# The high part of the mixers' weights: by a casting transfer on the gpsimd queue, or by a copy on the scalar or vector engine

## The chip, the cores and the metric

The kernel runs on one core of a Trainium2 chip. Its time is the device time of one execution in microseconds, from runs whose median is given. One execution was also taken by the hardware profiler; its page and trace are what this document reads. In the trace PE is TensorE's matmul, PEld its weight load, DVE is VectorE, ACT is ScalarE, POOL is GpSimd, SP is SyncE.

## What is computed

A two-layer network on 256 tokens of width 1024, in float32. Each layer is a half-weighted feed-forward block (SwiGLU, width 2816), a mixer, and another half-weighted feed-forward block, each followed by a residual sum with a factor and a layer normalisation:

```python
for layer in range(DEPTH):                      # DEPTH = 2, x: [1, 256, 1024]
    h = layer_norm(ALPHA * h + 0.5 * swiglu(h, ffn_w_in[layer, 0], ffn_w_out[layer, 0]), ...)
    if layer % 2 == 0:
        mix = hybrid_mixer(h, hyb_w_in, ..., hyb_w_out)      # [1024 x 5664] in, [2048 x 1024] out
    else:
        mix = nsa_mixer(h, positions, nsa_w_in, ..., nsa_w_out)  # [1024 x 1840] in, [1024 x 1024] out
    h = layer_norm(ALPHA * h + mix, ...)
    h = layer_norm(ALPHA * h + 0.5 * swiglu(h, ffn_w_in[layer, 1], ffn_w_out[layer, 1]), ...)
```

The hybrid mixer projects h, runs a causal convolution of length 4 over most of the columns, and then two branches beside each other: a gated delta rule (8 heads, solved in blocks) and a state-space scan (16 heads). Both are gated by a z projection and normalised, and go through one output projection. The NSA mixer is an attention of three branches (compressed blocks, selected blocks, window) with 16 query heads in 2 groups.

## The kernel before

**Three products for one.** TensorE runs the dense products in the type float32r, which keeps fewer bits than float32. To keep the accuracy, each dense weight tile is split in two: a high part `whi`, the weight rounded to float32r, and a low part `wlo`, the weight less its high part. The activations are split in the same way. A dense product is then three passes: high by high, high by low, low by high (`mm3`, lines 674 to 679).

**How a weight gets to TensorE.** `unit` (line 614) loads one weight unit of up to 128 x 2048 floats into a `raw` buffer by a transfer on SyncE's queue; there are 4 such buffers. It cuts the unit in parts of up to 128 x 1024 and for each part takes two buffers of the pool `m4`, `whi` and `wlo`, and calls `split` (line 608). `split` copies the part into `whi`, which rounds it. That copy is an operation with two possible engines: ScalarE's activation or VectorE's tensor_copy (`copy`, line 597). Then VectorE subtracts `whi` from the raw part into `wlo`. `unit_cols` (line 632) loads columns: each part is 128 columns for all 8 blocks of 128 rows, so in DRAM a partition's part lies in 8 runs of 512 bytes. `unit_rows` (line 638) loads rows of 512 or 1024 columns: a part is then 2 runs of 2 KB or 1 run of 4 KB for each partition. `tok_weights` (line 646) calls `unit_rows` for the z gates and the queries. The feed-forward blocks use `pair_weights` (line 654, with a split of its own) for their first tiles and `unit_cols` and `unit_rows` for the others. Two units of the mixers are loaded by direct calls of `unit`: the 32 small gate columns of the hybrid mixer (line 1068) and the key, value and gate columns of NSA (`chunk`, line 1578).

**Buffers.** `m4` has 36 buffers of 128 x 1024. Streams share it under quotas; the weight stream "W" may hold 12 while other streams have tiles pending that come before its own, and 24 otherwise. Within a stream, buffers are given in the order of first use in the program.

**What sets the order.** Nothing is issued directly. The program records operations in a `Plan`; `Plan.order` (line 315) then simulates a list schedule on five queues (tensor, vector, scalar, gpsimd, sync), with a price for each operation (`price`, line 239), latencies between engines, one shared DMA resource, buffers and PSUM banks. At each step it takes the operation that can start first, by program order where several can. An operation with two possible engines goes where it starts first. The result is one fixed order for each engine, which the hardware then follows with semaphores. So a change of a price or of an engine makes a new order for everything. Before, the price of every `dma_start` on its queue was 60 ns, and all were SyncE's.

**The mixers.** In the hybrid mixer the z gate of the delta branch (`z_gate`) and the key and query columns with their convolution (`gdn_conv`) come first; then five strands are woven by TensorE time (`weave`, line 729): the delta rule `delta`, the value columns and the state-space columns `space`, the second z gate `gate`, the scan `space2`, and the first half of the output projection `out_a`. The second half of it follows. GpSimd's part in it is small: triangular masks for the decays (`decays`, the tiles `bm`), inverse square roots by a power (`lnve` in the layer normalisation, `arena` elsewhere), and in NSA a few products (`tt`, which may also go to VectorE). No transfer is issued from GpSimd.

All operations are issued by one line (508), so the profile's lines are told apart by tile names, not by line numbers.

Of the kernel before, what the change touches and what calls it, by code (L numbers as in the profile page):

```python
# [9 lines left out]
F32 = mybir.dt.float32  # L10
# [3 lines left out]
OP = mybir.AluOpType  # L14
# [4 lines left out]
P = 128  # L19
# [142 lines left out]
class Plan:  # L162
# [76 lines left out]
    def price(self, op, eng, fn, args, kw):  # L239
        def n(a):  # L240
            return a.ids.size
        ps = lambda a: isinstance(a, V) and a.t.space == "PSUM"
        if eng == "tensor":
            out, l, r = args[:3]
            if fn == "transpose":
                return max(l.ids.size * 2, r.ids.size) / 2.4 + 2
            N, M = r.ids.size, l.ids.size
            if l.dtype == F32R:
                return N / 2.4 + (13.5 if M > 32 else 7)
            if M <= 32:  # L250
                return max(107.0, N * 0.42)
            if M <= 64:
                return 58.0 if N <= 64 else max(109.0, N * 0.84)
            return 4 * max(N, M) / 2.4 + 9
        if fn == "dma_start":
            return 60.0
        N = n(args[0]) if isinstance(args[0], V) else n(args[1])
        if isinstance(args[1] if len(args) > 1 else None, V):
            N = max(N, n(args[1]))
        ptr = sum(isinstance(kw.get(k), V) for k in ("scale", "bias"))  # L260
        if eng == "scalar":
            rows = args[0].p1 - args[0].p0

            more = (340 if rows <= 32 else 125 if rows <= 64 else 0) if fn == "activation" and N > 128 else 0
            return N / 1.2 + (51 if ps(args[1]) else 93) + 93 * ptr + (93 if "accum_out" in kw else 0) + more
        if eng == "vector":
            src = [a for a in args[1:] if isinstance(a, V)]
            if fn in ("tensor_copy", "tensor_scalar") and not any(ps(a) for a in src) and not ps(args[0]):
                c = N / (1.92 if N > 256 else 0.96) + 68
            elif fn == "reciprocal":  # L270
                c = N * 4 / 0.96 + 68
            elif fn == "memset":
                c = N / 0.96 + 20
            else:
                c = N / 0.96 + 67
            if fn == "scalar_tensor_tensor":
                c += 62 * isinstance(args[2], V)
            elif fn == "tensor_scalar":
                c += 62 * sum(isinstance(a, V) for a in args[2:4])
            return c  # L280
        if args[-1] is OP.pow:
            return 830.0 + 130.0 * N
        return max(250.0, {"tensor_tensor": N * 2.1 + 150, "memset": N * .83 + 36,
                           "affine_select": N * .9 + 180}.get(fn, N * 1.7 + 480))
# [247 lines left out]
class K:  # L532
# [78 lines left out]
        self.nc.vector.tensor_tensor(lo, src, hi.bitcast(F32), OP.subtract)  # L611


    def unit(self, srcs, parts):

        raw = self.plan.tile("raw", [P, 2048], F32, "raw", stream="W")
        for dst, src in srcs:
            self.nc.sync.dma_start(dst(raw), src)
        out = []
        for f in parts:  # L620
            v = f(raw)
            n = int(v.ids.size)
            shape = v.shape
            hi = self.m4(n, "whi", "W", F32R)
            lo = self.m4(n, "wlo", "W", F32R)
            if len(shape) == 3:
                hi, lo = (t.rearrange("p (a b) -> p a b", a=shape[1]) for t in (hi, lo))
            self.split(hi, lo, v)
            out.append((hi, lo))
        return out  # L630

    def unit_cols(self, w, c0, n):

        v3 = lambda r: r[:, :KD * n].rearrange("p (k n) -> p k n", k=KD)
        parts = [lambda r, e=e: v3(r)[:, :, e * P:(e + 1) * P] for e in range(n // P)]
        return self.unit([(v3, w[:, :, c0:c0 + n])], parts)

    def unit_rows(self, w, k0, nk, c0, n):

        v3 = lambda r: r[:, :nk * n].rearrange("p (k n) -> p k n", k=nk)  # L640
        g = min(nk, 1024 // n)
        out = self.unit([(v3, w[:, k0:k0 + nk, c0:c0 + n])],
                        [lambda r, e=e: v3(r)[:, e:e + g, :] for e in range(0, nk, g)])
        return [(hi[:, k, :], lo[:, k, :]) for hi, lo in out for k in range(g)]

    def tok_weights(self, w, c0, n):
# [187 lines left out]


    def ffn(self, l, j, x, then):
        nc = self.nc
        w_in = self.i['ffn_w_in'][l, j].rearrange("(k p) n -> p k n", p=P)
        w_out = self.i['ffn_w_out'][l, j].rearrange("(k p) n -> p k n", p=P)
# [7 lines left out]
        def gtiles(f):  # L847
            if f // 2 not in pairs:
                pairs[f // 2] = self.m4(1024, "g", "G", F32R).rearrange("p (a t) -> p a t", a=4)
            v = pairs[f // 2]  # L850
            return v[:, f % 2 * 2, :], v[:, f % 2 * 2 + 1, :]
# [55 lines left out]
        for s in range(NT, DFF // 256):  # L907
# [8 lines left out]
            for e in range(2):  # L916
                if e == 1:
                    wo = self.unit_rows(w_out, 2 * s, 2, 0, D)
                f = 2 * s + e
# [5 lines left out]
                g = gtiles(f)  # L925
# [105 lines left out]

    def hybrid(self, x, then):
        self.arena = None
        nc, i = self.nc, self.i
        V = nc.vector
        w_in = i['hyb_w_in'][0].rearrange("(k p) n -> p k n", p=P)
# [30 lines left out]
        v3 = lambda r: r[:, :256].rearrange("p (k n) -> p k n", k=KD)  # L1067
# [32 lines left out]
        g = self.sm([P, 2, 24], "g24")  # L1100
# [453 lines left out]

    def nsa(self, x, then):
        self.arena = None
        nc, i = self.nc, self.i
        V = nc.vector
        w_in = i['nsa_w_in'][0].rearrange("(k p) n -> p k n", p=P)
# [427 lines left out]
```

## Time and profile before

| | |
|---|---|
| Median of 3 runs | 1137.44 us (1136.66 to 1139.3) |
| Span of the profiled execution | 1135.9 us |
| Mean granted TensorE clock | 0.997 of full speed |
| Busy: PE / DVE / ACT / POOL | 1113.5 / 892.4 / 510.4 / 66.6 us |
| Bytes moved by DMA, mean rate | 198.37 MB, 175 GB/s |
| First feed-forward block | about 0 to 194 us |
| Hybrid mixer | about 194 to 446 us |
| Second and third feed-forward block | about 446 to 806 us |
| NSA mixer | about 806 to 945 us |
| Last feed-forward block | about 945 to 1136 us |

The profiled execution's own time is its span, from the first instruction to the last; it stands 1.5 us below the median of the runs, in which the launch and the end are counted too. A row of a group reads: line, engine, operation, output <- inputs by tile name, partitions x elements, xcount | busy time in us, mean ns of one | idle time of the engine just before them, and what ended it. A row of the chain reads: start in us, length in us, what. A row of the waits reads: who waited <- for whom: us in total, times, the longest. A row of the issues reads: destination <- source, queue, xcount, KB each, median us from issue to landing.

### The profile page before, as it was taken

How to read it: one execution, taken by the hardware profiler on the slowest of the kernel's cores; microseconds unless marked ns; L12 is line 12 of the kernel's file. 1: busy time of each engine (PE TensorE's matmuls, PEld its weight loads, DVE VectorE, ACT ScalarE, POOL GpSimd, SP SyncE). 2: the span in 40 equal slices, each digit the busy share in tenths (PEclk: the TensorE clock that was granted, in tenths of full speed). 3: DMA queues.
4: the chain of work that ended last, by engine and by line, in shares of the span. 5: the costliest groups of instructions: out<-in, count | busy, mean ns of one | idle time of the engine just before them, and what ended most of it. 6: DMA issues, size and time to landing. Idle time of an engine off the chain costs nothing.

```text
span 1135.9 us, 16503 instructions
## 1 busy us (share of the span) xinstructions
PE 1113.5 (98%) x6558; PEld 947.8 (83%) x6558; DVE 892.4 (79%) x1495; ACT 510.4 (45%) x909; POOL 66.6 (6%) x101
## 2 busy tenths in 40 slices
PE   9999999999999999999999999999999999999997
PEld 6888888898999778888888888888877668888886
DVE  7977778789979998777768967775869789777755
ACT  6644332378545655533333633342346556433320
POOL 1000000021011410000000000000101210000000
PEclk9999999999999999999999999999999999999999
DMA  9966552544632275755563765546336217655510
GB/s 331 337 209 207 188 198 84 177 131 128 220 123 75 78 268 175 257 198 180 185 215 112 270 211 188 188 153 190 111 105 229 75 40 270 238 194 185 185 38 37
DMA packets 150678, 198.37 MB, mean 175 GB/s; under 512 B 9389, under 2 KB 127562, under 8 KB 150602
## 3 DMA queue, kind: packets, MB, share of 16 engines
q1 hardware_dynamic: 150602, 197.33, 52.1%
q8 instruction: 51, 0.84, 0.3%
q14 instruction: 25, 0.20, 0.0%
HBM read 194.04 MB, written 1.05 MB: 172 GB/s over the span
## 4 chain that ended last, share of the span: by engine, by line
PE 88%; DVE 8%; ACT 2%; issue 1%; DMA 0%; POOL 0%; SPq 0%; DVEq 0%; ACTq 0%
PE ps L508 53%; PE acc L508 30%; PE mp L508 5%; DVE wlo L508 2%; DVE arena L508 1%; DVE cv L508 1%; DVE qs L508 1%; DVE P L508 1%; DMA raw<-in_ffn_w_in_dram 0%; ACT P L508 0%; DVE AT L508 0%; DVE h L508 0%; DVE x L508 0%; DVE whi L508 0%; DVE kd L508 0%
## 5 line engine op out<-in xcount | busy, mean ns | idle before, releaser
L508 DVE TENSOR_TENSOR wlo<-raw,whi 128x1024 fp32r<-128x1024 f32 (+1 forms) x349 | 416.7, 1214 | 8.6 <-ACT whi L508 5.7
L508 PE MATMUL ps<-x,whi 128*128 128x512 f32 (+1 forms) x1616 | 376.7, 363 | 0.7 <-ACT cv L508 0.5
L508 PEld LDWEIGHTS ps<-x,whi 128*128 128x128 f32 x1616 | 284.2, 188 | 45.8 <-ACT cv L508 1.8
L508 ACT ACTIVATE whi<-raw 128x1024 fp32r<-128x1024 f32 x255 | 256.9, 1049 | 15.8 <-DMA raw<-in_ffn_w_in_dram 10.5
L508 PE MATMUL acc<-whi,g 128*128 128x512 f32 x704 | 230.7, 391 | 0.0
L508 PE MATMUL ps<-x,wlo 128*128 128x256 f32 x1400 | 227.0, 283 | 1.5 <-DVE wlo L508 1.5
L508 ACT ACTIVATE sg<-ps 128x256 f32<-128x256 f32 x162 | 62.2, 384 | 352.3 <-PE ps L508 352.2
L508 PEld LDWEIGHTS ps<-x,wlo 128*128 128x128 f32 x1400 | 201.9, 190 | 14.0 <-DVE wlo L508 1.7
L508 DVE TENSOR_TENSOR sg<-ps,sg 128x256 f32<-128x256 f32 x162 | 68.7, 424 | 161.8 <-ACT sg L508 161.6
L508 PEld LDWEIGHTS acc<-whi,g 128*128 128x128 f32 x704 | 132.5, 188 | 25.9
L508 PE MATMUL acc<-wlo,g 128*128 128x512 f32 x352 | 138.1, 392 | 0.0
L508 PE MATMUL ps<-whi,x 128*128 128x512 f32 (+1 forms) x480 | 129.8, 386 | 1.2 <-DVE whi L508 1.2
L508 PEld LDWEIGHTS ps<-whi,x 128*128 128x128 f32 x480 | 86.1, 188 | 17.8 <-DVE whi L508 2.0
L508 PEld LDWEIGHTS acc<-wlo,g 128*128 128x128 f32 x352 | 66.4, 189 | 10.9
L508 PE MATMUL ps<-wlo,x 128*128 128x512 f32 (+1 forms) x240 | 68.0, 381 | 0.5 <-DVE wlo L508 0.5
L508 DVE CAST whi<-raw 128x1024 fp32r<-128x1024 f32 (+2 forms) x94 | 63.8, 681 | 5.0 <-DMA raw<-in_nsa_w_in_dram 3.9
L508 PE MATMUL acc<-whi,x 128*128 128x512 f32 x192 | 63.9, 403 | 0.1
L508 POOL TENSOR_TENSOR lnve<-lnve,mhalf 128x1 f32<-128x1 f32 x12 | 11.5, 957 | 706.4 <-DVE lnve L508 706.4
L508 PEld LDWEIGHTS ps<-wlo,x 128*128 128x128 f32 x240 | 43.2, 188 | 8.1 <-DVE wlo L508 1.2
L508 ACT ACTIVATE sg<-sg 128x256 f32<-128x256 f32 x74 | 30.9, 418 | 33.9 <-DVE sg L508 33.9
L508 DVE SCALAR_TENSOR_TENSOR cv<-cv,arena 128x255 f32<-128x255 f32 (+2 forms) x84 | 41.3, 494 | 1.3 <-ACT cv L508 0.6
L508 PEld LDWEIGHTS acc<-whi,x 128*128 128x128 f32 x192 | 35.5, 188 | 8.1 <-issue 1.1
(254 smaller groups left out, 1011.0 us busy)
## 6 DMA issues: line engine op xcount, KB each, us to landing
raw<-in_ffn_w_in_dram SPq DMA_DIRECT2D x74, 1024.0 KB, 5.1
raw<-in_ffn_w_out_dram SPq DMA_DIRECT2D x44, 1024.0 KB, 4.9
raw<-in_hyb_w_in_dram SPq DMA_DIRECT2D x20, 1024.0 KB, 5.1
raw<-in_ffn_w_in_dram SPq DMA_DIRECT2D x24, 512.0 KB, 4.3
raw<-in_hyb_w_out_dram SPq DMA_DIRECT2D x8, 1024.0 KB, 4.9
raw<-in_nsa_w_in_dram SPq DMA_DIRECT2D x5, 1024.0 KB, 5.0
raw<-in_nsa_cmp_w_dram SPq DMA_DIRECT2D x4, 1024.0 KB, 5.3
raw<-in_nsa_w_out_dram SPq DMA_DIRECT2D x4, 1024.0 KB, 7.6
```

The lines of the kernel that those rows point to most:

```text
L508: r = getattr(getattr(nc, eng), fn)(*[res(a) for a in args], **{k: res(a) for k, a in kw.items()})
```

## The change

In both mixers the high part of a dense weight no longer comes from the raw tile by a copy on ScalarE or VectorE. Instead, a transfer on GpSimd's queue reads the same weight from DRAM a second time and writes it into `whi`; as the destination is float32r and the source float32, the transfer converts. The low part is still VectorE's subtraction, now of the raw tile and the transferred high part. `unit_cols` and `unit_rows` pass the DRAM slices (`heads`). A flag `mixing` is set in the mixers and cleared in the feed-forward blocks, which keep the copy, as do the two direct calls of `unit`. The planner's price of a `dma_start` on GpSimd's queue is 1000 ns.

```diff
@@ Plan.price
         if fn == "dma_start":
-            return 60.0
+            return 1000.0 if eng == "gpsimd" else 60.0
@@ K
-    def unit(self, srcs, parts):
+    def unit(self, srcs, parts, heads=None):
 
         raw = self.plan.tile("raw", [P, 2048], F32, "raw", stream="W")
         for dst, src in srcs:
             self.nc.sync.dma_start(dst(raw), src)
         out = []
-        for f in parts:
+        for m, f in enumerate(parts):
             v = f(raw)
...
-            self.split(hi, lo, v)
+            if self.mixing and heads:
+                self.nc.gpsimd.dma_start(hi, heads[m])
+                self.nc.vector.tensor_tensor(lo, v, hi.bitcast(F32), OP.subtract)
+            else:
+                self.split(hi, lo, v)
             out.append((hi, lo))
         return out
@@ unit_cols
-        return self.unit([(v3, w[:, :, c0:c0 + n])], parts)
+        heads = [w[:, :, c0 + e * P:c0 + (e + 1) * P] for e in range(n // P)]
+        return self.unit([(v3, w[:, :, c0:c0 + n])], parts, heads)
@@ unit_rows
         out = self.unit([(v3, w[:, k0:k0 + nk, c0:c0 + n])],
-                        [lambda r, e=e: v3(r)[:, e:e + g, :] for e in range(0, nk, g)])
+                        [lambda r, e=e: v3(r)[:, e:e + g, :] for e in range(0, nk, g)],
+                        [w[:, k0 + e:k0 + e + g, c0:c0 + n] for e in range(0, nk, g)])
@@ ffn
+        self.mixing = False
@@ hybrid and nsa
+        self.mixing = True
```

More of the change, by code (lines that the diff above doesn't have):

```diff
@@ L1556, in nsa @@
         self.arena = None
+        self.mixing = True
         nc, i = self.nc, self.i
```

## The prediction

> **What bounds the kernel now.** I read the page's head first, then the stretches of time by stage, then the chain of waits in the two mixers, and last the groups, the waits and the issues.
>
> ```profile
> span 1135.9 us, 16503 instructions
> PE 1113.5 (98%) x6558; PEld 947.8 (83%) x6558; DVE 892.4 (79%) x1495; ACT 510.4 (45%) x909; POOL 66.6 (6%) x101
> q1 hardware_dynamic: 150602, 197.33, 52.1%
> ```
>
> TensorE is busy nearly all the time, so only time that TensorE loses can be won back. The span is 1135.9 us; the runs' median is 1137.44 us, 1.5 us more, and I carry these 1.5 us along. Next the stretches: the hybrid mixer runs from about 194 to 446 us, the NSA mixer from about 806 to 945 us.
>
> ```profile
> core 0: us, PE busy (x) PEld busy (x) DVE busy (x) ACT busy (x) POOL busy (x), PEclk, DMA share, GB/s
> 155.00:310.00 155.00, 153.57 (x1109) 137.76 (x1107) 133.98 (x283) 83.40 (x142) 13.07 (x12) 1.00 0.49 152
> 194.00:446.00 252.00, 249.62 (x1937) 219.84 (x1936) 228.95 (x437) 140.05 (x223) 39.29 (x51) 1.00 0.46 152
> 806.00:945.00 139.00, 129.39 (x816) 100.71 (x815) 113.19 (x211) 72.93 (x205) 16.70 (x21) 0.99 0.36 123
> ```
>
> TensorE stands visibly idle for 252 - 249.62 = 2.4 us in the hybrid mixer and 139 - 129.39 = 9.6 us in NSA: 12.0 us together. DVE is the second engine (229 of 252 us, 113 of 139 us), ACT has room, POOL is nearly free. The chain of waits in the same two stretches, hybrid first:
>
> ```profile
> by line: PE ps L508 38.7%; PE acc L508 27.6%; PE mp L508 8.7%; DVE wlo L508 6.0%; DVE cv L508 3.3%; issue 1.7%; DVE AT L508 1.7%; DVE arena L508 1.3%; DVE x L508 1.1%; DVE y L508 1.0%; DVE XT L508 0.9%; DVE kq L508 0.8%; ACT sw L508 0.8%; D
> by line: PE acc L508 23.7%; PE ps L508 23.2%; PE mp L508 17.2%; DVE qs L508 5.7%; DVE wlo L508 4.7%; DVE P L508 4.6%; DVE arena L508 4.3%; ACT P L508 3.3%; DVE kd L508 1.4%; DVE PT L508 1.4%; DVE whi L508 1.4%; issue 1.3%; DVE h L508 1.0%;
> ```
>
> The subtraction that makes the low part (wlo) is the largest piece that is not TensorE: 6.0% of 252 = 15.1 us and 4.7% of 139 = 6.5 us. The copy that makes the high part (whi) is hardly there.
>
> **The change, part by part.** How many copies go follows from the issues of the weights.
>
> ```profile
> raw<-in_hyb_w_in_dram SPq DMA_DIRECT2D x20, 1024.0 KB, 5.1
> raw<-in_hyb_w_out_dram SPq DMA_DIRECT2D x8, 1024.0 KB, 4.9
> raw<-in_nsa_w_in_dram SPq DMA_DIRECT2D x5, 1024.0 KB, 5.0
> raw<-in_nsa_w_out_dram SPq DMA_DIRECT2D x4, 1024.0 KB, 7.6
> raw<-in_hyb_w_in_dram SPq DMA_DIRECT2D x4, 512.0 KB, 3.6
> ```
>
> Each 1024 KB unit has two parts of 128x1024, each 512 KB unit one: 2 x 28 + 4 = 60 parts in the hybrid mixer and 2 x 9 = 18 in NSA, so 78 copies go and 78 transfers of 512 KB on POOL's queue come. The 32 gate columns and NSA's key and value chunks give no source for the high part and keep their copies. What the copies cost, hybrid first, then NSA (feed-forward weights prepared in these stretches are among them):
>
> ```profile
> L508 ACT ACTIVATE whi<-raw 128x1024 fp32r<-128x1024 f32 x49 | 50.1, 1050 | 5.6 <-DMA raw<-in_ffn_w_in_dram 4.1 <-PE ps L508 1.4
> L508 DVE CAST whi<-raw 128x1024 fp32r<-128x1024 f32 x15 | 10.7, 713 | 0.0
> L508 DVE TENSOR_TENSOR wlo<-raw,whi 128x1024 fp32r<-128x1024 f32 x64 | 77.9, 1227 | 0.9 <-ACT whi L508 0.5
> L508 ACT ACTIVATE whi<-raw 128x1024 fp32r<-128x1024 f32 x19 | 19.3, 1051 | 4.2 <-DMA raw<-in_nsa_w_in_dram 2.4 <-DMA raw<-in_nsa_w_out_dram 1.0 <-DMA raw<-in_ffn_w_in_dram 0.8
> L508 DVE CAST whi<-raw 128x1024 fp32r<-128x1024 f32 x7 | 4.8, 698 | 3.9 <-DMA raw<-in_nsa_w_in_dram 3.9
> ```
>
> ACT loses up to 50 + 19 us and DVE up to 10.7 + 4.8 us of work; the subtractions, 1.2 us each on the busier DVE, all stay. Most of what goes lies beside TensorE. What lies on the path: the copies in the chain, and TensorE's waits for ACT work that stands in the queue with such copies.
>
> ```profile
> 272.53 0.78 ACT whi L508
> 377.70 0.96 ACT whi L508
> 404.45 0.60 DVE whi L508
> 829.91 1.21 DVE whi L508 x2
> 862.03 0.69 DVE whi L508
> PE ps L508 <- ACT cv L508: 0.5, 1, 0.5
> PEld ps L508 <- ACT cv L508: 1.8, 5, 1.0
> PEld mp L508 <- ACT vT L508: 0.6, 1, 0.6
> PEld mp L508 <- ACT xT L508: 0.4, 1, 0.4
> ```
>
> **Gain.** The five pieces sum to 4.2 us; the waits to 3.3 us, of which I take half, since the convolution's own work ends them too. Together -6 us. The bounds are 0 and the 12.0 us that TensorE stands idle.
>
> **The later high part.** The copy yields the high part 1.05 us after its raw tile is there. A transfer can start when the slot is free, without the raw tile, but needs at least the 3.6 us of the 512 KB row: up to 3.6 - 1.05 = 2.55 us later wherever the slot came free only just in time. Who waits is wlo, and behind it in DVE's queue the convolution's sums, the delta rule and the normalisation. On the chain stand about 15.1 / 1.23 = 12 wlo in hybrid and 5 in NSA, 17 in all. The bounds are 0 (all fetched ahead) and 17 x 2.55 = 43 us.
>
> ```profile
> SPq L508 <- DVE wlo L508: 804.4, 149, 21.5
> 210.00:220.00 10.00, 10.00 (x60) 8.61 (x59) 5.41 (x7) 2.48 (x3) 0.00 (x0) 1.00 0.84 287
> 222.94 2.88 PE acc L508 x24
> L508 SPq DMA_DIRECT2D raw<-in_hyb_w_in_dram x18: 367/368/380, 196.7 to 306.8; - x18
> ```
>
> SyncE's queue waits 804 us in all for wlo to give back raw buffers, so fetching ahead is limited by buffers and not by transfers; yet the copies in hybrid waited for no raw tile of hybrid weights (their idle time names ffn_w_in alone). Nearer the low end, then: I let one in five of the 17 wait, about 3.5, and 3.5 x 2.55 = +9 us.
>
> **DMA share.** Queue q1 moves 197.33 MB in 52.1% of 1135.9 us: 333 GB/s at full share, so a part (128 x 1024 x 4 bytes = 0.524 MB) takes 1.57 us. Sixty take 94 us, and the hybrid share goes from 0.46 to 0.46 + 94 / 252 = 0.83. The 44 parts of the input projection (16 by rows for the two gates, 28 by columns), loaded between 155 and 310 us, take 69 us of 155: 0.49 + 0.45 = 0.94. That cover is nearly used up: raw tiles will land later than 5.1 us, and zero-fills and normalisation rows with them. At 0.84 (the stretch from 210 us) TensorE was still busy 10.00 of 10, so the price is small: I take +2 us, between 0 and the 10 us by which 0.94 of 155 us misses a full queue.
>
> **POOL's queue.**
>
> ```profile
> L508 POOL TENSOR_SCALAR_AFFINE_SELECT bm<-arena 128x512 fp32r<-128x512 f32 x24 | 22.3, 957 | 128.5 <-PE acc L508 67.4 <-DVE arena L508 39.0 <-PE ps L508 18.0
> L508 POOL TENSOR_TENSOR P<-P,arena 128x1024 f32<-128x1024 f32 x5 | 10.3, 2075 | 39.7 <-DVE arena L508 27.9 <-ACT PT L508 11.8
> L508 POOL TENSOR_TENSOR lnve<-lnve,mhalf 128x1 f32<-128x1 f32 x12 | 11.5, 957 | 706.4 <-DVE lnve L508 706.4
> ```
>
> No transfer is issued from POOL in this trace. The nearest rows bound an issue by SyncE's 0.37 us and by POOL's pass over 1024 columns, 2.08 us; I take 1 us, which is also what the planner is now told. 60 us fit beside 39.29 in 252. But POOL works in order: a transfer that waits for a slot holds up the decay masks (bm) and the powers (lnve, arena) behind it, and TensorE and DVE wait for those. One issue ahead of one power on the path: +1 us, between 0 and six powers at the borders of the mixers by 2.08 us, 12 us. SyncE's queue loses nothing and gets nothing.
>
> **The planner.** The new price of 1000 and the shorter ACT and DVE work give a new order on all engines. I set it at zero; by the idle of the mixers it can win no more than the 12.0 us.
>
> **Sum:** -6 + 9 + 2 + 1 = +6 us, and 1137.4 + 6 = 1143 us. Alone, this case reaches from 1140 to 1155.
>
> **A rule beside this.** The Trainium skill, "DMA: Bandwidth & Descriptors", section "Latency and other measured facts", puts the first byte of a transfer from SyncE or ACT at about 0.6 us and of one from GpSimd at about 1 us, since software writes its descriptors. By that estimate each of the 3.5 waits is 0.4 us longer and the sum is 1145 us; no trace here shows a GpSimd transfer yet.
>
> **Rivals.**
>
> **Faster, 1131 us.** The high parts are issued far enough ahead, since they need a slot but no raw tile, that no wlo on the chain waits. Only the gain stays, with the small terms hidden too: 1137.4 - 6. For it: POOL is free 84% of the hybrid stretch, and raw tiles of hybrid weights were never late. Against it: slots come free at TensorE's pace, and a high part now holds its slot some 2.5 us longer. It decides where fewer than 1.2 of the 17 wait (1.2 x 2.55 = 3 us, what the gain leaves after the two small terms).
>
> **POOL's issue becomes the bound, 1169 us.** A column part is 128 partitions by 8 rows: 1,024 runs of 512 bytes, where a row part has 128 or 256 runs. TensorE consumes a part in 2.88 us (24 products at 222.94). Were an issue of 1,024 runs longer than that, POOL would set the pace of the 28 column parts: at 4 us, 28 x 1.12 = 31 us. For it: the number of runs. Against it: the nearest rows end at 2.08 us. The Trainium skill, "SBUF — State Buffer", section "A bandwidth-pool intuition that's wrong (but worth ruling out)", adds that a DVE copy in its two-port mode keeps GpSimd from writing descriptors. One cast of 0.71 us per issue would lower the threshold to 2.17 us; but the 15 casts of the hybrid row mostly go with the change.
>
> **No change, 1137 us.** Waits and gain cancel, or the planner puts the freed time where TensorE has none to win. For it: TensorE busy 249.62 of 252.
>
> **How the numbers follow.** Forecast 0.36, POOL as the bound 0.16, faster 0.35, no change 0.13. A measurement here can tell about 0.2% (2.3 us) from nothing. Slower is the first two together, 0.52. The range goes down to 1128, the gain of 6 us and half of what it lacks to its bound, and up to 1170, the POOL case; outside I leave about 0.05 below and 0.10 above.
>
> **What would show it.** Right: about 78 transfers on a new queue of some 41 MB; ACT's whi groups in the two stretches down to the feed-forward and chunk weights; DMA share near 0.8 in hybrid; DVE idle ahead of wlo, released by the high part's transfer, some 10 us in sum; TensorE's hybrid stretch 4 to 8 us longer, NSA about even. Wrong toward faster: wlo waits for raw or for nothing. Wrong toward much slower: POOL busy over 2.9 us for a column transfer, or a high part that lands over 6 us after its issue even where the queue is quiet, which would mean that the casting itself is slow.

## The result, and the profile after

The changed kernel takes 1153.0 us (median of 4 runs, 1152.75 to 1153.83); before took 1137.8 us beside it (1136.66 to 1139.3). The ratio is 1.0137, with a 95% interval of 1.0125 to 1.0149: slower by 15 us. The profiled execution took 1153.1 us.

The head of the page of after:

```profile
span 1151.4 us, 16651 instructions
PE 1120.2 (97%) x6558; PEld 951.5 (83%) x6558; DVE 877.2 (76%) x1459; ACT 461.8 (40%) x863; POOL 119.3 (10%) x183
...
q1 hardware_dynamic: 150602, 197.33, 51.4%
q0 software_dynamic: 41184, 40.90, 16.7%
```

The change did what it says. ACT has 49 us less work and DVE 15 us less, and a new queue moves 40.90 MB (78 x 0.524). Yet TensorE, with the same 6558 products, is busy 6.7 us longer (1120.2 against 1113.5). Busy time of equal work grows only if single products get longer, so the clock has to be looked at.

Next the stretches of time, the two mixers from layer norm to layer norm, first before, then after (columns as in the prediction's rows):

```profile
197.70:441.60 243.90, 241.52 (x1897) 213.03 (x1897) 220.92 (x424) 137.08 (x217) 38.34 (x51) 1.00 0.46 150
812.10:949.90 137.80, 128.19 (x792) 98.71 (x791) 111.99 (x208) 71.75 (x200) 16.74 (x22) 0.99 0.38 131
```

```profile
198.10:461.90 263.80, 248.06 (x1897) 217.34 (x1896) 214.44 (x408) 103.32 (x182) 76.91 (x103) 0.97 0.99 242
832.40:963.50 131.10, 125.56 (x781) 95.74 (x780) 105.73 (x193) 65.95 (x197) 21.89 (x39) 1.00 0.61 197
```

The hybrid mixer lost 19.9 us (263.8 - 243.9), NSA won 6.7 us; part of that is a shifted border, since the stretch holds 781 products against 792. From NSA's first border to the end of the span, after is 4.8 us shorter (319.0 against 323.8). The four feed-forward blocks, from layer norm to layer norm, differ by 1.8 us together. Of the hybrid mixer's 19.9 us, 6.5 are TensorE's longer busy time (248.06 - 241.52, the same 1897 products), and 13.4 are idle time (15.7 against 2.4). The granted clock in the hybrid stage fell from 1.00 to 0.97. Where it fell, in stretches of 5 us of after:

```profile
305.00:310.00 5.00, 4.45 (x95) 3.83 (x95) 4.72 (x11) 1.68 (x5) 0.87 (x1) 1.00 1.31 322
310.00:315.00 5.00, 5.00 (x66) 4.94 (x63) 3.95 (x6) 0.00 (x0) 0.88 (x1) 0.53 1.92 315
315.00:320.00 5.00, 5.00 (x105) 4.52 (x105) 2.55 (x6) 0.98 (x2) 0.87 (x1) 0.79 1.42 342
...
430.00:435.00 5.00, 1.89 (x7) 1.72 (x8) 5.00 (x6) 0.60 (x1) 1.48 (x1) 0.50 0.52 163
435.00:440.00 5.00, 5.00 (x21) 4.02 (x20) 4.97 (x7) 1.36 (x2) 0.00 (x0) 0.84 1.06 350
```

A reader who looks at the PE column alone sees a full engine from 310 to 320 us; the column before the DMA share says that it ran at 0.53 and 0.79 of its speed. (The DMA share adds up the time of packets in flight, so it can pass 1.) By an estimate from these rows, the first place loses 5 x 0.47 + 5 x 0.21 = 3.4 us of TensorE's work, the second 1.89 x 0.50 + 5 x 0.16 = 1.7 us: 5.1 of the 6.5 us.

The waits of after in 194 to 446 us (engine, what it waited to do, for whom: us in sum, times, longest), to be held against the 3.3 us of TensorE's waits on ACT in the prediction's rows:

```profile
ACT whi L508 <- DMA raw<-in_ffn_w_in_dram: 14.7, 4, 8.5
...
PE mp L508 <- DVE y L508: 6.7, 3, 5.9
...
DVE whi L508 <- DMA raw<-in_ffn_w_in_dram: 6.2, 1, 6.2
DVE wlo L508 <- DMA whi<-in_hyb_w_in_dram: 5.8, 7, 3.0
PEld ps L508 <- ACT cv L508: 4.8, 7, 1.6
PEld ps L508 <- DVE wlo L508: 4.2, 4, 2.1
...
PE ps L508 <- DMA whi<-in_hyb_w_in_dram: 2.7, 3, 1.4
```

Two kinds stand out: high parts that land late for the subtraction and for TensorE, and one wait of 5.9 us for the scan's y, with ACT and DVE held by a raw tile of the next feed-forward. POOL as the one waited for hardly appears: 1.2 us for a power and 0.7 us for the decay masks. What the transfers themselves took, from the list of POOL's high-part instructions (duration of the issue: shortest, median, longest in ns) and from the issues' landing times (KB, median us):

```profile
L508 POOL DMA_DIRECT2D whi<-in_hyb_w_in_dram x44: 698/873/934, 155.9 to 354.0; - x44
L508 POOL DMA_DIRECT2D whi<-in_hyb_w_out_dram x16: 535/562/595, 355.4 to 415.4; - x16
...
DMA to landing us min/median/max: 3.5/6.2/14.7
```

```profile
whi<-in_hyb_w_in_dram POOLq DMA_DIRECT2D x44, 512.0 KB, 7.1
raw<-in_hyb_w_in_dram SPq DMA_DIRECT2D x20, 1024.0 KB, 6.0
...
whi<-in_hyb_w_out_dram POOLq DMA_DIRECT2D x16, 512.0 KB, 5.9
```

An issue costs 0.56 to 0.87 us in the median. The quickest landing is 3.5 us, where SyncE's 512 KB row in the prediction has 3.6 us in the median, so the casting is not slow. The median in the input projection is 7.1 us.

### The profile page after: what moved, and what is told of

Its sections match the earlier page's. It is cut to its first block, busy times and chain, and to the rows that moved or that the text cites. A ratio compares the mean times of both kernels' runs of the same rounds, so it can differ in the third digit from the quotient of the medians.

```text
span 1151.4 us, 16651 instructions
## 1 busy us (share of the span) xinstructions
PE 1120.2 (97%) x6558; PEld 951.5 (83%) x6558; DVE 877.2 (76%) x1459; ACT 461.8 (40%) x863; POOL 119.3 (10%) x183
## 3 DMA queue, kind: packets, MB, share of 16 engines
q0 software_dynamic: 41184, 40.90, 16.7%
HBM read 234.93 MB, written 1.05 MB: 205 GB/s over the span
## 5 line engine op out<-in xcount | busy, mean ns | idle before, releaser
L508 ACT ACTIVATE whi<-raw 128x1024 fp32r<-128x1024 f32 (+1 forms) x196 | 196.7, 1050 | 24.1 <-DMA raw<-in_ffn_w_in_dram 23.4
L508 PEld LDWEIGHTS acc<-whi,g 128*128 128x128 f32 x704 | 132.5, 188 | 25.9
L508 PE MATMUL acc<-wlo,g 128*128 128x512 f32 x352 | 138.0, 392 | 0.0
L508 PEld LDWEIGHTS ps<-whi,x 128*128 128x128 f32 x480 | 86.1, 188 | 17.1 <-DVE x L508 1.2
L508 POOL DMA_DIRECT2D whi<-in_hyb_w_in_dram x44 | 36.4, 829 | 245.7 <-PE ps L508 192.7
L508 DVE CAST whi<-raw 128x1024 fp32r<-128x1024 f32 (+2 forms) x75 | 50.4, 674 | 6.2 <-DMA raw<-in_ffn_w_in_dram 6.2
```

The costliest lines, as they stand in the source:

```text
L508: r = getattr(getattr(nc, eng), fn)(*[res(a) for a in args], **{k: res(a) for k, a in kw.items()})
```

## The experiments

At first three theories stood. **A:** the transfers crowd the DMA engines in the hybrid mixer. **B:** any transfer on POOL's queue costs. **O:** the planner's new order loses the time, or leans on early landings. They were tried in that order; a fourth, **L** (too little lead), came out of it. Lead is the time between the release of the buffer, the slot, that a high part goes into and the subtraction that reads the high part. All stage times come from the one profiled execution of each run, which lay up to 3.2 us off the run's median, so a stage difference of 2 or 3 us says little by itself. The kernel before measured 1136.9 to 1137.6 us beside them.

| run | hybrid us | NSA us | kernel us | ratio to before, 95% |
|---|---|---|---|---|
| before | 243.9 | 137.8 | 1137.8 | |
| after | 263.8 | 131.1 | 1153.0 | 1.0125 to 1.0149 |
| NSA only | 243.8 | 132.5 | 1133.5 | 0.9959 to 0.9979 |
| hybrid only | 261.5 | 133.2 | 1154.5 | 1.013 to 1.019 |
| later landing planned | 272.1 | 140.0 | 1168.6 | 1.0262 to 1.0293 |
| extra bytes on SyncE | 259.4 | 137.3 | 1197.6 | 1.0509 to 1.0546 |
| after's order, copies | 261.7 | 137.5 | 1157.0 | 1.0159 to 1.0202 |
| the same, copies earlier | 267.5 | 137.4 | 1160.2 | 1.0161 to 1.0224 |
| extra bytes on POOL | 272.6 | 137.6 | 1167.8 | 1.0252 to 1.0289 |
| NSA + output projection | 251.9 | 131.0 | 1141.2 | 1.0021 to 1.0047 |
| NSA + gate rows | 245.6 | 131.0 | 1135.6 | 0.9973 to 0.9992 |
| before's order, transfers | 260.2 | 139.1 | 1156.3 | 1.013 to 1.0189 |
| bytes unknown to planner | 266.9 | 131.8 | 1160.4 | 1.0168 to 1.0211 |
| long lead only | 244.7 | 137.8 | 1138.8 | 0.9999 to 1.0021 |
| short lead only | 256.6 | 138.0 | 1150.4 | 1.0087 to 1.0146 |
| tail reordered | 259.0 | 131.0 | 1147.2 | 1.006 to 1.0099 |
| near parts copied | 253.7 | 132.6 | 1141.9 | 1.0025 to 1.005 |
| far parts only | 244.2 | 131.0 | 1135.1 | 0.9972 to 0.9991 |

**Which mixer.** After, with the flag off in one mixer:

```diff
     def hybrid(self, x, then):
-        self.mixing = True
+        self.mixing = False
```

> The transfer in NSA alone (18 parts), the hybrid mixer keeps its copies. By the powers of the layer normalisations the changed kernel takes 131.1 us for the NSA mixer where the kernel before takes 137.8. Theory A (the hybrid mixer carries all of the loss, 263.8 against 243.9 us, because its transfers ask for more than the DMA engines give): the two mixers are independent, so this kernel is 6 to 7 us faster than before, about 1131 us. Theory B (the loss comes with any transfer on the gpsimd queue, NSA's gain is a shift between stages): no faster than before, 1137 us or more.

```diff
     def nsa(self, x, then):
-        self.mixing = True
+        self.mixing = False
```

> The transfer in the hybrid mixer alone (60 parts). Theory A: the whole loss without NSA's gain, about 20 us over the kernel before, 1157 to 1159 us, hybrid stage near 264 us. Theory B: between the kernel before and the changed one, 1145 to 1150 us.

NSA alone: 1133.5 us (1132.9 to 1135.0), 3.4 us faster than before and the best version found. Hybrid alone: 1154.5 us (1151.7 to 1160.2). So B falls: with 18 transfers on POOL's queue the kernel is no slower. The loss is the hybrid mixer's. But the transfers are not shown to be what NSA gains by. In hybrid alone, NSA kept all its copies, planned anew, and still took 133.2 us against 137.8 before, with the same products (791 in this trace, 792 in before's); from its first border to the end of the span it was 319.7 us, against 319.0 in after and 323.8 before. NSA in hybrid alone:

```profile
830.30:963.50 133.20, 126.21 (x791) 97.53 (x790) 111.46 (x201) 71.49 (x201) 15.56 (x27) 1.00 0.39 131
```

**The planner's view of landing.**

```diff
-                op.end = dma_free + 600
+                op.end = dma_free + (3600 if e == "gpsimd" else 600)
```

> The changed kernel with one number of the planner changed: a transfer of the gpsimd queue is taken to land 3 us later. The transfers and their bytes stay, only the order is made for late landings. Rival theory O (the order is at fault: it puts the subtraction where the plan believes that the high part has landed, 3.8 us after issue, and it lands after 7): most of the loss goes, below 1145 us. Theory A (the DMA engines cannot deliver in time, whatever the order): within 4 us of the changed kernel, 1149 to 1157 us.

1168.6 us, hybrid 272.1 us: told that casting transfers land 3 us later, the planner finds a worse order, not a safer one. Neither expectation held. The same transfers cost 16 us more in another order, so the order does matter. Its opposite, where the casting transfers count no bytes:

```diff
-                op.nbytes = (a.p1 - a.p0) * a.ids.size * 4
+                op.nbytes = 0 if op.eng == "gpsimd" else (a.p1 - a.p0) * a.ids.size * 4
```

> After, with one change in the planner: the casting transfers count no bytes in its model of the DMA engines (their issue on POOL still counts 1 us). They all still run. If the order is bad because the planner makes raw tiles late behind the casting transfers: the hybrid stage falls by 5 us or more, the kernel to 1138 to 1148 us. If the transfers cost the time on the chip, an order that takes them for free is no better: the hybrid stage 260 to 275 us, the kernel 1150 to 1165 us.

1160.4 us, hybrid 266.9 us, as expected if the transfers cost the time on the chip. Neither change repairs the stage.

**Bytes alone, two attempts.** Before's order and copies, with the parts read a second time into spare buffers (both edits also shrink a scratch size of the program, from 4096 to 1024 and to 2048), first on SyncE:

```diff
+            for h in heads:
+                k, c = h.shape[1:]
+                for e in range(4):
+                    dum = self.plan.tile("dum", [P, 256], F32, "dum")
...
+                    self.nc.sync.dma_start(dum.rearrange("p (a b) -> p a b", a=max(1, k // 4)), part)
```

> The kernel before, in its own order and with its copies, but in the hybrid mixer the same DRAM slices are read a second time into spare buffers that nothing reads, by SyncE's queue, in pieces of 128 KB right behind each raw tile (31 MB more). No wait on a high part, no work on GpSimd, no freed ACT. Theory A in its pure form (bytes alone make raw tiles, zero fills and normalisation rows late): 8 to 20 us slower than before, 1145 to 1157 us. Theory O or a theory that the wait for the high part itself is the cost: within 4 us of before, 1137 to 1141 us.

1197.6 us, but 46 us of it were lost ahead of the hybrid mixer. The spare transfers waited for nothing, so they were issued from 8.5 us on, in SyncE's row, ahead of raw tiles. The run decides nothing. Then on POOL's queue, held back by the copy:

```diff
+                        d = beside.tile([P, 512], mybir.dt.bfloat16, name=f"dum_{count}", tag="dum")
...
+                        if e == 0:
+                            nc.gpsimd.tensor_copy(d[:, :1], res(args[0].t.view())[:, :1].bitcast(F32))
+                        nc.gpsimd.dma_start(d.rearrange("p (a b) -> p a b", a=part.shape[1]), part)
```

> Before's order and before's copies. Behind each copy of a hybrid high part POOL's queue reads the same 512 KB of weights a second time, in two casting transfers (to bf16) into spare buffers that nothing reads; POOL waits for the copy first, so that the transfers spread as the parts do. 60 parts, 31 MB. Theory A1 (crowded DMA engines make the raw tiles, zero-fills and rows late): the hybrid stage grows from 243.9 us to 255 to 265 us, the kernel to 1147 to 1158 us. Theory A2 (the subtraction's wait for its own transfer costs the time, and the other transfers do not matter): the hybrid stage stays within 3 us of 243.9 us, the kernel at 1136 to 1141 us.

1167.8 us, more than either theory gave, by another way. Among the waits of this run are:

```profile
POOL dum L517 <- ACT whi L508: 23.6, 13, 4.2
...
DVE y L508 <- POOL arena L508: 12.1, 3, 9.1
...
PEld acc L508 <- POOL bm L508: 9.1, 6, 6.1
```

POOL, standing in order behind its wait for the copy, was late with the power (arena) for y and with the decay masks (bm). It says nothing of the bytes. It does show what a wait at the head of POOL's queue can cost; in after the waits for POOL are the 1.2 and 0.7 us named above.

**Order against transfers.** After's order on every engine, without transfers, the high parts made by copies set into ACT's row:

```diff
+                first, hi = todo.pop(id(args[2].t))
+                at = n
+                while at > first + 1 and self.starts[at - 1] >= self.starts[n] - 1500.0:
+                    at -= 1
+                put.setdefault(at, []).append(("scalar", "activation", (hi, args[1], AF.Copy), {}))
...
+            if not (op[0] == "gpsimd" and op[1] == "dma_start"):
+                out.append(op)
```

> After's order on every engine, but each of the 78 casting transfers is left out and a copy on ACT makes the high part, set into ACT's row 1.5 us of planned time ahead of the subtraction that reads it. No byte more than before moves. Theory A (the transfers themselves cost the time): the hybrid stage, 263.8 us in after, goes back to 244 to 248 us, and the whole kernel to 1131 to 1140 us. Theory O (the new order alone costs it): the hybrid stage stays at 258 to 266 us and the kernel at 1147 to 1156 us.

1157.0 us, hybrid 261.7 us: about theory O's numbers. But the subtraction waited 17.1 us for the unplanned copies, so it was tried with the copies up to 5 us ahead:

```diff
+                due = max(landed[id(args[1].t)], self.starts[n] - 5000.0)
...
-                while at > first + 1 and self.starts[at - 1] >= self.starts[n] - 1500.0:
+                while at > first + 1 and self.starts[at - 1] >= due:
```

> As the run of after's order with copies on ACT in place of the transfers, which came to 1157 us with 17.1 us of waits of the subtraction for ACT's copy; here each copy stands in ACT's row up to 5 us ahead of its subtraction (not before the raw tile's planned landing). Theory O (after's order itself loses the time): the hybrid stage stays at 256 to 264 us, the kernel at 1146 to 1157 us, though the wait for the copies goes. If the first run was slow only because its copies came late, the hybrid stage falls to 243 to 249 us and the kernel to 1135 to 1142 us.

1160.2 us, hybrid 267.5 us, above both expectations, and still 11.9 us of waits for the copies. These two hold an order that was not made for the copies, and can't say what it costs with what it was made for. The other half says more: before's order kept, the copies taken out, transfers put in where the slot comes free:

```diff
+                gone.add(n)
+                at = n
+                while at > 0 and self.starts[at - 1] >= args[0].t.slot_free:
+                    at -= 1
+                put.setdefault(at, []).append(("gpsimd", "dma_start", (args[0], head), {}))
```

> Before's order on PE, DVE, ACT and SyncE, kept operation for operation; only the 78 copies of the mixers' high parts are taken out and a casting transfer on POOL's queue is put in for each, at the planned time at which its slot comes free (6 to 27 us ahead of the subtraction for most parts, 1 to 6 us for about 15 of them, planned between 272 and 345 us). Theory A (the transfers cost the time, by crowding and late landing): the hybrid stage, 243.9 us in before and 263.8 us in after, comes to 258 to 268 us, the kernel to 1147 to 1160 us. Theory O (the new order costs it): the hybrid stage stays at 241 to 247 us and the kernel at 1130 to 1140 us. In between, both have a share.

1156.3 us (1153.2 to 1158.6), hybrid 260.2 us. Nothing is added but transfers, ACT and DVE have less to do, and the stage loses 16.3 us. So the transfers in an unchanged order are enough for such a loss. That after's order adds nothing is not shown, and before's order was not made for transfers either.

**Where in the stage.** The flag as a set of allowed shapes; in hybrid (1,), the output projection alone, then (2,), the gate rows alone:

```diff
-            if self.mixing and heads:
+            if heads and heads[m].shape[1] in self.mixing:
...
-        self.mixing = True
+        self.mixing = (1,)
```

> The change in NSA and, in the hybrid mixer, for the 16 parts of the output projection alone; the 44 parts of the input projection keep their copies. NSA alone gave 1133.5 us. If the 20 us of the hybrid stage go by the number of parts: 16/60 of 20 = +5, 1139 us. If the burst of six casting issues at the stage's end is what cost the 8 us there: 1141 us. If only the crowded input projection pays: 1133 to 1134 us.

> The change in NSA and, in the hybrid mixer, for the 16 parts by rows of the two gates alone; the 28 column parts and the 16 of the output projection keep their copies. By the number of parts: +5, 1139 us. If the crowded stretch of column parts alone pays: 1133 to 1134 us. If the landing of any part that is needed soon pays, 1137 to 1143 us.

The output projection's 16 parts cost 8.1 us of hybrid time (251.9), the number that the burst theory gave (1141 us, measured 1141.2). The place is only in part the one it gave: TensorE's added idle time lies between 380 and 395 us (2.2 us) as well as between 425 and 445 us (2.5 us), all at a clock of 1.00. The 16 gate rows, in a lighter stretch, cost about 2 us. By subtraction the 28 column parts cost about 10.

**Lead against bytes.** A copy needs its slot 1 us before the subtraction, a transfer 4 us in a quiet queue and 7 in a full one. So the parts were split by the planned time from the slot's release to the subtraction, in before's order (here 8 us or more; the second run has the opposite sign, and neither has transfers in NSA):

```diff
-            if head is not None:
+            if head is not None and due[id(args[0].t)] - args[0].t.slot_free >= 8000.0:
```

> Before's order, NSA as before, and in the hybrid mixer casting transfers in place of the copies for only the 41 parts whose slot comes free 8 us or more (planned) ahead of the subtraction that reads them; the 19 others keep their copies. All 60 and NSA's 18 gave a hybrid stage of 260.2 us (before 243.9). Theory L (a high part that lands too late for its own subtraction): the stage stays within 3 us of 243.9, the kernel at 1136 to 1140 us. Theory C (the bytes crowd the DMA engines and make raw tiles and rows late): 41/60 of +16 us, 252 to 258 us, the kernel 1145 to 1152 us.

> The complement: before's order, NSA as before, casting transfers only for the 19 parts whose slot comes free less than 8 us ahead of the subtraction, 16 of them planned between 272 and 346 us. 10 MB. Theory L (late for the own subtraction): the hybrid stage loses most of the 16 us, 254 to 262 us, the kernel 1147 to 1156 us. Theory C (bytes): 19/60 of +16 us, 247 to 250 us, the kernel 1141 to 1144 us.

Long lead, 41 parts, 21.5 MB: 1138.8 us (1138.2 to 1140.3), no different from before by the interval. Short lead, 19 parts, 10.0 MB: 1150.4 us (1149.9 to 1154.0). Half the bytes of the long-lead run, and most of the loss (12.7 of the 16.3 us of hybrid time). The hybrid stage and the landing of its high parts, long lead first, then short lead (its landing for the 11 parts issued between 270 and 345 us):

```profile
198.60:443.30 244.70, 240.48 (x1893) 212.19 (x1892) 212.52 (x409) 117.21 (x195) 59.98 (x82) 1.00 0.81 218
```

```profile
DMA to landing us min/median/max: 3.9/7.0/18.5
```

```profile
197.50:454.10 256.60, 243.69 (x1898) 214.24 (x1897) 220.83 (x423) 123.15 (x202) 50.83 (x66) 0.99 0.65 175
```

```profile
DMA to landing us min/median/max: 4.1/8.1/10.7
```

With long lead the DMA share is 0.81 and parts land after up to 18.5 us, and TensorE hardly notices: the clock is 1.00. With short lead the share of the whole stage is lower and the loss is there. That alone does not clear the bytes: the short-lead parts lie close together, and between 270 and 345 us the share was 0.59 with long lead, which has only 3 parts there, and 1.00 with short lead:

```profile
270.00:345.00 75.00, 74.39 (x897) 70.24 (x897) 66.57 (x140) 41.22 (x74) 7.28 (x7) 1.00 0.59 166
```

```profile
270.00:345.00 75.00, 64.63 (x803) 59.94 (x802) 56.89 (x124) 25.71 (x53) 11.22 (x14) 0.95 1.00 211
```

What tells is the chain of waits of the short-lead run in 270 to 330 us. It waits for the parts' own transfers, and no piece of it is a raw tile:

```profile
by line: DMA whi<-in_hyb_w_in_dram 22.3%; PE ps L526 18.7%; PE acc L526 16.8%; DVE wlo L526 10.9%; DVE cv L526 9.0%; DVE sw L526 6.9%; issue 6.8%; ACT Y L526 2.1%; DVE DT L526 1.9%; DVE XT L526 1.5%; PE mp L526 1.3%; ACT vT L526 0.7%; ACT X
...
280.21 4.67 DMA whi<-in_hyb_w_in_dram
...
289.73 6.85 PE ps L526 x51
296.64 0.61 DVE wlo L526
297.25 8.70 DMA whi<-in_hyb_w_in_dram
```

22.3% of 60 us is 13.4 us, two transfers of 4.67 and 8.70 us. The second starts where TensorE's product and a subtraction have just given a buffer back: slot, transfer, subtraction and product stand in a ring, and the transfer puts 8.7 us into it where a copy puts 1.05. Theory L holds in before's order, with the crowd of transfers at that place as what makes each landing long.

**The end of the stage.** In after, DVE at the end of the scan (start, us, what, idle ahead of it), and then ACT, PE:

```profile
421.13 0.68 DVE L508 TENSOR_TENSOR y<-y,zs 128x512 f32<-128x512 f32 x1
428.02 0.69 DVE L508 CAST whi<-raw 128x1024 fp32r<-128x1024 f32 x1 [6.21 <-DMA raw<-in_ffn_w_in_dram]
...
432.22 0.75 DVE L508 SCALAR_TENSOR_TENSOR y<-y,arena,snw 128x512 f32<-128x512 f32 x1
```

```profile
428.15 1.06 ACT L508 ACTIVATE whi<-raw 128x1024 fp32r<-128x1024 f32 x1 [8.46 <-DMA raw<-in_ffn_w_in_dram]
429.12 0.61 ACT L508 ACTIVATE ysq<-y 128x512 f32<-128x512 f32 x1
```

```profile
433.11 1.09 PE L508 MATMUL mp<-ident,y 128*128 128x128 f32 x4 [5.87 <-DVE y L508]
```

Six casting transfers are issued back to back, five of them begun before that raw tile's issue at 414.99 us:

```profile
412.70 3.24 POOL L508 DMA_DIRECT2D whi<-in_hyb_w_out_dram  x6
```

The raw tile (512 KB) landed 11.6 us after its issue, where the median of the feed-forward's 512 KB tiles in after is 4.7. The next feed-forward's first copies wait for it in ACT's and DVE's rows, and the square of y, ready at 421.8 us, stands behind them until 429.12. TensorE waits 5.87 us for y and comes back at a clock of 0.50. After, with the three instructions that wait for the raw tile set behind the scan's last y:

```diff
+        return ([o for n, o in enumerate(order[:last + 1]) if n not in keep] + [order[n] for n in late]
+                + order[last + 1:])
```

> After, with three instructions moved: the next feed-forward's first copy on ACT, its first copy on DVE and one subtraction, which wait for a late raw tile, stand behind the scan's last y multiply instead of ahead of it. If that in-order wait and the clock that falls behind it cost the time at the hybrid stage's end: TensorE's idle of 5.9 us ahead of the y transposes falls under 2 us, the granted clock of 0.67 between 430 and 440 us goes back to 0.95 or more, and the kernel comes to 1142 to 1147 us. If the late raw tile only makes TensorE wait a little later: 1150 to 1153 us.

1147.2 us (1146.4 to 1147.7), 5.8 us less than after, just outside the 1142 to 1147 us expected; TensorE's stretch is full and at speed:

```profile
430.00:440.00 10.00, 10.00 (x46) 8.27 (x45) 9.93 (x11) 3.59 (x4) 0.00 (x0) 1.00 0.81 247
...
440.00:450.00 10.00, 7.91 (x40) 6.36 (x39) 9.90 (x15) 4.50 (x6) 0.99 (x1) 1.00 1.00 345
```

Some of it comes back at 440 us, where TensorE is idle for 2.1 us.

**In after's own order.** Planned anew, with the 18 hybrid parts back on copies whose slots come free late (columns from 1792, last gate's rows), and then the output projection's 16 too:

```diff
+    def near(self, h):
+        return h.tensor.name == "in_hyb_w_in_dram" and h.shape[1] in (2, 8) and (
+            h.offset % h.ap[0][0] in range(1792, 2048) or h.offset % h.ap[0][0] >= 3600)
...
-            if self.mixing and heads:
+            if self.mixing and heads and not self.near(heads[m]):
```

> After, planned anew, with 18 of the 60 hybrid parts back on copies: the columns from 1792 on and the last gate's rows from 3600 on, whose slots after's plan frees mostly 5 to 10 us ahead of their subtractions, between 270 and 345 us. 42 hybrid parts and NSA's 18 stay transfers. If the short lead costs the time in after's order too: the loss between 250 and 340 us goes (about 10 us of the 20), the stage's end keeps its own, the hybrid stage 249 to 254 us and the kernel 1139 to 1144 us. If the bytes count: 42/60 of 20 us, 257 to 259 us, the kernel 1146 to 1149 us.

```diff
-        return h.tensor.name == "in_hyb_w_in_dram" and h.shape[1] in (2, 8) and (
+        return h.tensor.name == "in_hyb_w_out_dram" or h.tensor.name == "in_hyb_w_in_dram" and h.shape[1] in (2, 8) and (
```

> As the run before, with the 16 parts of the output projection back on copies too, so that the burst of casting issues at the stage's end is gone: 26 hybrid parts, all with 10 us or more of lead, and NSA's 18. If short lead and the burst at the end are the whole cause: the hybrid stage 243 to 247 us and the kernel 1132 to 1137 us, as with NSA alone (1133.5 us). If the bytes count: 26/60 of 20 us, 252 us, the kernel 1141 us.

1141.9 us (1141.0 to 1145.0) and 1135.1 us (1134.2 to 1136.9): both inside what L and the burst expect, and below what the bytes expect. So of the 18 us between 1135.1 and 1153.0, 11 go with the parts with a short lead and 7 with the output projection, each taken back in an order planned anew. The 26 far parts that stay win nothing over NSA alone (1133.5).

## Why the prediction was wrong

The forecast was 1143 us, 6 us slower: the direction and the range (1128 to 1170) held, the size, 15 us, did not. What failed are two terms. The price of a crowded DMA at the stage's end, held in "+2", was 7 us. The later high part, "+9", was 11 to 13 us, made of fewer and much longer waits than the sum has. Beside them the gain, 6 us, was 3.4 us where the change was in NSA alone, and came another way. By its steps:

- **Gain, -6 us.** It did not come from the missing copies. I took it from pieces in the chain of both mixers, and wrote that NSA would come out about even. In the hybrid mixer there was none to see: 41 copies less gave +0.8 us. NSA won 6.7 us as a stage and 3.4 us alone in the whole kernel, but with transfers in before's order it took 139.1 us, and with its copies kept, in the new order of hybrid alone, 133.2 us, most of the way from 137.8 to after's 131.1. So the new order gave most of it: the planner's share, which I had set at zero. That this order came out well for NSA is luck as far as the runs show, since the one with later landing planned took 140.0 us.
- **The later high part, +9 us: the price of a wait failed.** The sum has 3.5 waits of 2.55 us. The price rested on the 3.6 us of landing of SyncE's row before the change; the median in the hybrid input projection was 7.1 us, which is 6 us later than a copy, not 2.55. The count rested on "the copies in hybrid waited for no raw tile", which speaks of the raw tile's lead. A transfer into `whi` doesn't wait for that; it waits for the slot, as the prediction says itself, and slots come free at TensorE's pace where the delta rule is at work. Most such parts lie close together between 270 and 345 us. Measured: 11 to 13 us, by the short-lead run and by taking those parts back. In the short-lead run's chain it is two waits, of 4.67 and 8.70 us. That +9 came so near is partly luck: the sum has too many waits, each of them too cheap. The sign named for it, some 10 us of DVE's idle time released by the transfer, was 5.8 us in after.
- **DMA share, +2 us: the step that missed most.** I forecast a share of 0.83; it was 0.99. As a cost by itself it showed nothing up to 0.81, with long lead. Nor is 1 the limit that I took it for: between 155 and 310 us, where I forecast 0.94, it was 1.16. Its effect lies in the landing times, that is, in the term before, and in the burst at the stage's end: 7 us, through raw tiles of the next feed-forward that I said "will land later" and then priced at nearly nothing. Three runs give that size: 5.8 us by moving three instructions, 6.8 by taking the output projection's parts back, 7.6 by adding them to NSA alone.
- **The clock: missing.** A part of the losses is no wait at all but slower products, 6.5 us in the hybrid stage. The Trainium skill, "TensorE: Matmul & The Clock Gate", section "Why this matters for your kernels", asks for no idle gaps beyond about 3 us between products, since one idle window brings the clock down to half. The trace agrees for the long gap: 5.87 us of idle, then 0.50. It would have told me that a long wait costs more than its own length. As a limit it is not sharp here: 1.86 us of idle were followed by 0.50 in the run with near parts copied, and 3.03 us were not in after's order with copies.
- **POOL's queue, +1 us.** Right: 0.56 to 0.87 us for an issue where I took 1, and in the hybrid stretch of after the longest sum of waits for POOL was 1.2 us (DVE, for a power). The rival that POOL sets the pace falls: it needed more than 2.88 us.
- **The rule of the first byte**, which gave 1145 us, doesn't decide it: the quickest casting transfer landed after 3.5 us, and SyncE's 512 KB took 3.6 in the median before. What hurt is a rule that the prediction left out. The Trainium skill, "DMA: Bandwidth & Descriptors", section "Issuing engines are not separate DMA queues", says that transfers of all queues share the same 16 engines and interleave. The trace agrees: SyncE's raw tile amid six of POOL's transfers took 11.6 us.
- **Faster (1131 us)** did not come true. The change in NSA alone took 1133.5 us, but the runs lay most of that to the order and not to its reason, the missing copies. Its condition, fewer than 1.2 late parts, was the right question. The prediction even names the slots against it, but it set the count by the raw tiles and not by the buffers of the pool.

What stays open: how after's order by itself compares with before's, since the two runs with copies in it had work that it was not planned for; and how much of the 11 to 13 us is too little lead and how much the crowding of transfers at one place, since most parts with a short lead lie there; in after, 3.4 us of slower products go with the order, as the last section shows.

## What to carry to other kernels

When a copy becomes a transfer into the same buffer, ask how long before its reader that buffer comes free, not when the source is there: 41 transfers with 8 us or more of planned lead cost nothing here, at a DMA share of 0.81, while of 19 with less, two put their whole landing time into the ring of buffers. Price landing at the load that the change itself makes, and look for what stands in order behind the transfers that become later. Count a wait of several microseconds of TensorE twice: once for the wait, once for the clock after it. And where a change makes a new order, do not credit the change with what the order did: compare a part of the kernel that the change left alone, as NSA in hybrid alone.

## What the runs showed of the hardware

The clock fell in a stretch with hardly a gap, too. In after, TensorE between 306 and 312 us (PE's rows):

```profile
306.27 1.12 PE L508 MATMUL acc<-XT,AT 64*64 64x32 f32 x32
307.32 0.39 PE L508 MATMUL ps<-x,wlo 128*128 128x256 f32 x1
...
309.78 1.48 PE L508 MATMUL acc<-Y,XT 64*64 64x32 f32 x32
311.07 1.48 PE L508 MATMUL acc<-XT,AT 64*64 64x32 f32 x22
312.48 0.58 PE L508 MATMUL ps<-x,whi 128*128 128x256 f32 x1
```

From 306.27 to 312.48 us there were nearly only products of 64 x 64 by 32 columns, with one idle gap of 0.54 us. In stretches of 1 us, the granted clock was 1.00 up to 310 us, 0.65 from 310 to 311 and 0.50 from there to 317, with TensorE "busy" all the time from 309 us on. Nothing waited ahead of the dense product at 312.48, so it is after's order that puts the small products together; before's order has dense products between them at 305.0 and 309.9 us, and its clock was 1.00 through the whole stage. The run of after's order with copies, which has no casting transfers, falls to 0.50 at the same products (from 312 us). So the clock's loss at this place, 3.4 us by the estimate above, goes with the order and not with a late transfer. That small products are the reason is the likely reading; no run tests it alone.

After idle time the picture is this. In the hybrid stages of all runs, each of ten gaps of 4.3 us or more was followed by a clock of 0.50. Gaps between 1.6 and 3.3 us went either way: 1.86 us, then 0.50, with near parts copied; 2.33 us, then 0.50, with the tail reordered; 3.03 us at 1.00 throughout in after's order with copies. In this stretch of after 2 us of idle time left the clock alone, but in pieces of which the longest was 0.88 us:

```profile
390.00:400.00 10.00, 8.01 (x39) 5.52 (x38) 9.96 (x18) 4.10 (x6) 10.00 (x26) 1.00 0.80 258
```

A casting transfer from float32 to float32r has no price of its own that shows (3.5 us for 512 KB at best), and POOL's issue grows little with the number of runs: 0.56 us for 128, 0.87 us for 1,024.
